# A 2048-cube matmul with layer norm: the first four row tiles cut one quarter to three quarters along k, and the row means of B written one tile earlier

## The chip, the cores and the metric

The kernel runs on one core of a Trainium2 chip. The metric is device time in microseconds (us) for one execution of the whole program. The engines named below: PE multiplies matrices, DVE (VectorE) and ACT (ScalarE) work elementwise, POOL (GpSimd) here mostly issues DMAs, SP (SyncE) only issues DMAs. PE writes into PSUM, which has eight banks of 128 x 512 f32; DVE and ACT move results out of it.

## The reference

```python
x = np.matmul(a, b)                     # a, b: 2048 x 2048 f32
mean = np.mean(x, axis=-1, keepdims=True)
var = np.var(x, axis=-1, keepdims=True)
normalized = (x - mean) / np.sqrt(var + eps)
return (gamma * normalized + beta).astype(np.float32)
```

## The kernel before

A is cut into 16 row tiles of 128 rows (i or g), k into 16 blocks of 128 (kt or t), the columns of B into four groups of 512 (q; q 0 and 1 are the left half, 2 and 3 the right). One product of PE (`mm`, L136 to L140) multiplies one k block of one row tile, transposed, with 512 columns of B into one PSUM bank. There are 15 x 4 x 16 = 960 of them; the last row tile is done apart with other widths (`products_last`, L219).

All data come as f32 and are cast to f16. B comes in half rows: `load_b(kt, h)` (L74) loads 128 x 1024 f32 (512 KB) of k block kt, left (h 0) or right (h 1), into one of eight slots (`bigp`), named w{kt}_{h}. `cast_left` and `cast_right` (L79, L84) cast 512 columns each on DVE and ACT into the resident `b16`, which frees the slot.

The first four row tiles (G = 4) are handled apart, since PE could otherwise do little until all of B is there. Their A comes in 16 pieces n of 128 rows x 512 of k (256 KB), four row tiles for each quarter c of k: `load_first(n)` (L91) loads it into a slot of `firstp` (four slots, each as large as half a row tile), `cast_first` (L97) casts it on DVE, `turn_first` (L102) transposes it on PE into a PSUM bank (four small matmuls), `keep_first` (L107) copies it from there on DVE into `at[g]`. The later row tiles come as two halves of eight DMAs of 64 KB (`load_tile`, L111), are cast on ACT (`cast_tile`, L119) and transposed on DVE (`transpose_part`, L127).

Four row tiles times two column groups fill the eight banks, and one bank is needed for the pieces being transposed. So the start goes in four stages: left columns over k blocks 0 to 7, right columns over 0 to 7, left columns over 8 to 15, right columns over 8 to 15. In the first two, seven banks (`early`) are filled while the pieces are transposed through the eighth; then the eighth (`late`) is filled too. `put_by` (L147) copies a bank's half sum to SBUF on ACT (f32, 16 copies in all), which frees the bank for the next stage; `add_up` (L151) in the last two stages adds the second part to it on DVE; `stats` (L142) then takes the statistics.

After that each row tile goes through all of k for four banks in turn (L442 to L460), DVE takes statistics, centres and scales (`normalise`, L184), SP stores. The results of the first four tiles are normalised beside the products of tiles 4 to 11.

The last tile needs its row mean early. For that the row means of B are appended to b16 as two more columns: `sum_b` (L206) sums the rows of b16 on ACT during tiles 6 to 13, `mean_b` (L211) makes of it, with four small DVE instructions and 16 small ACT copies (L217), the columns N and N+1 of b16, which the first products of the last tile read.

The order on every engine is the order of the program text (a schedule written out by hand). Each engine works in order, so an instruction that waits holds back all behind it on its engine. A DMA on a queue waits for the slot it fills and for the DMA eight before it in the program. At the very start PE does products on zeros (`warm_up`, L297) as fillers.

Of the kernel before, what the change touches and what calls it, by code (L numbers as in the profile page):

```python
# [15 lines left out]
def kernel(  # L16
# [57 lines left out]
    def load_b(kt, h, queue=None):  # L74
        w = bigp.tile([P, NH], FP32, tag="big", name=f"w{kt}_{h}")
        (queue or nc.sync).dma_start(w, b_rows[kt // 4, kt % 4][:, ds(h * NH, NH)])
        b_in[kt, h] = w
# [12 lines left out]

    def load_first(n):  # L91
        g, c = pieces[n]
        f = firstp.tile([P, 4 * P], FP32, tag="first", name=f"f{g}_{c}")
        nc.sync.dma_start(f, a[ts(g, P), ts(c, 4 * P)])  # L94
        a_in[n] = f

    def cast_first(n):  # L97
        h = first16.tile([P, P, 4], FP16, tag="h", name=f"h{n}")
        nc.vector.tensor_copy(h.rearrange("m p t -> m (p t)"), a_in[n])  # L99
        a_in[n] = h  # L100

    def turn_first(n):  # L102
        t_of[n] = psum.tile([P, 4, P], FP16, tag="c_ps", bufs=8, name=f"t_ps{n}")
        for t in range(4):
            nc.tensor.transpose(t_of[n][:, t, :], a_in[n][:, :, t], ident)  # L105
# [5 lines left out]
    def load_tile(i, h, queue):  # L111
        f = firstp.tile([P, 2, 4, P], FP32, tag="first", name=f"p{i}_{h}")
        for c in (0, 1):
            for q in range(4):
                queue.dma_start(  # L115
                    f[ds(32 * q, 32), c], a_pieces[q, 2 * h + c][:, ds(4 * i, 4)])
        tile_in[i, h] = f
# [6 lines left out]
    def new_at(i):  # L124
        at[i] = atp.tile([P, n_kt, P], FP16, tag="at", name=f"at{i}")
# [7 lines left out]
    def bank(i, q):  # L133
        x_of[i, q] = psum.tile([P, NB], FP32, tag="c_ps", bufs=8, name=f"ps_{i}_{q}")
# [11 lines left out]

    def put_by(i, q):  # L147
        part[i, q] = xpool.tile([P, NB], FP32, tag="x_sb", name=f"x_{i}_{q}")
        nc.scalar.copy(part[i, q], x_of[i, q])  # L149

    def add_up(i, q):  # L151
        x = part[i, q]
# [138 lines left out]
    with tc.manual_schedule(engines=order):  # L291
        nc.vector.memset(warm, 0.0)
        nc.vector.memset(ident, 0.0)
        nc.vector.memset(eps_t, float(eps))
        w_ps = psum.tile([P, NB], FP32, tag="c_ps", bufs=8, name="w_ps")

        def warm_up(n):  # L297
            for _ in range(n):
                nc.tensor.matmul(w_ps, warm[:, 0:P], warm, start=True, stop=True)

        nc.gpsimd.affine_select(
            out=ident, in_=ident, compare_op=AluOp.not_equal, fill=1.0,
            base=0, pattern=[[-1, P]], channel_multiplier=1,
        )
        KH = n_kt // 2
        load_first(0)
        load_b(0, 0, nc.scalar)
        load_first(1)
        for n in range(1, KH):
            load_first(n + 1)  # L310
            load_b(n, 0)
        for t in range(KH):
            load_b(t, 1)
            if KH + t + 1 < n_kt:
                load_first(KH + t + 1)
        for t in range(KH, n_kt):
            load_b(t, 0)
        for t in range(KH, n_kt):
            load_b(t, 1)
        for i in (4, 5):  # L320
            for h in (0, 1):
                load_tile(i, h, nc.sync)
        nc.sync.dma_start(gamma_b, gamma.unsqueeze(0).to_broadcast([P, N]))
        nc.sync.dma_start(beta_b, beta.unsqueeze(0).to_broadcast([P, N]))
        for i in range(6, n_mt):
            for h in (0, 1):
                load_tile(i, h, nc.gpsimd)

        left = [(g, q) for g in range(G) for q in (0, 1)]
        right = [(g, q) for g in range(G) for q in (2, 3)]  # L330
        early, late = left[:-1], left[-1]
        for g in range(G):
            new_at(g)


        warm_up(10)
        cast_first(0)
        turn_first(0)
        cast_first(1)
        warm_up(2)  # L340
        for n in range(KH):
            g, c = pieces[n]
            keep_first(n)
            cast_left(n)
            cast_first(n + 2)
            if n + 1 < KH:
                turn_first(n + 1)
            if n in (0, 1, 2):
                warm_up((3, 3, 2)[n])
            if c == 0:  # L350
                for x in early:
                    if x[0] == g:
                        bank(*x)
            if n == KH - 1:
                break
            for t in range(g + 1):
                for gg, q in early:
                    if gg <= g and (gg == g or t == g):
                        mm(gg, q, 4 * c + t, 0, KH)
        bank(*late)  # L360
        cast_right(0)
        for g, q in early:
            for t in range(4 if g == 3 else KH - 1, KH):
                mm(g, q, t, 0, KH)
            put_by(g, q)
            if (g, q) == (1, 1):
                cast_right(1)
        for t in range(KH):
            mm(*late, t, 0, KH)
        cast_right(2)  # L370
        put_by(*late)


        early, late = right[:-1], right[-1]
        for g, q in early:
            bank(g, q)
        for t in range(KH):
            n = KH + t
            turn_first(n)
            if t > 2:  # L380
                cast_right(t)
            keep_first(n)
            if n + 2 < n_kt:
                cast_first(n + 2)
            if t < KH - 2:
                for g, q in early:
                    mm(g, q, t, 0, KH)
        bank(*late)
        for t in range(KH, KH + 2):
            cast_left(t)  # L390
        for g, q in early:
            for t in (KH - 2, KH - 1):
                mm(g, q, t, 0, KH)
            put_by(g, q)
        for t in range(KH):
            mm(*late, t, 0, KH)
        put_by(*late)
        for t in range(KH + 2, n_kt):
            cast_left(t)


        for g, q in left:
            bank(g, q)
        for t in range(KH, KH + 3):
            for g, q in left:
                mm(g, q, t, KH)
        for j, (g, q) in enumerate(left):
            for t in range(KH + 3, n_kt):
                mm(g, q, t, KH)
            add_up(g, q)  # L410
            if j % 2 and j < 6:
                cast_right(KH + j // 2)


        for g, q in right:
            bank(g, q)
        for t in range(KH + 3, n_kt):
            cast_right(t)
            stats(*left[t - KH - 3])
        for g, q in left[5:]:  # L420
            stats(g, q)
        for t in range(KH, n_kt - 2):
            for g, q in right:
                mm(g, q, t, KH)
        new_at(4)
        for h in (0, 1):
            cast_tile(4, h)
            transpose_part(4, 2 * h)
            transpose_part(4, 2 * h + 1)
        for g, q in right:  # L430
            for t in (n_kt - 2, n_kt - 1):
                mm(g, q, t, KH)
            add_up(g, q)
        for g, q in right:
            stats(g, q)
        new_at(5)
        for c in range(4):
            if c % 2 == 0:
                cast_tile(5, c // 2)
            transpose_part(5, c)  # L440

        for i in range(G, last):  # L442
            if i == 6:
                junk = xpool.tile([P, 2 * NB], FP16, tag="x_sb", name="junk")
            if i > G:
                normalise(i - 1)
            if i + 2 < n_mt:
                new_at(i + 2)
            for q in range(n_nb):
                bank(i, q)  # L450
                for t in range(n_kt):
                    mm(i, q, t)
                stats(i, q)
                if i + 2 < n_mt:
                    if q % 2 == 0:
                        cast_tile(i + 2, q // 2)
                    transpose_part(i + 2, q)
                if 6 <= i < 14:
                    sum_b(4 * (i - 6) + q, junk)
                if q == 3 and i < 3 * G:  # L460
                    normalise((i - G) // 2, (i - G) % 2)
        mean_b()
        normalise(last - 1)
        for j in range(len(spans)):
            products_last(j)
            if j == 0:
                mean_last()
            stats_last(j)
            if j < len(spans) - 2:
                centre_last(j)  # L470
        finish_last()
# [31 lines left out]
```

## Time and profile before

| | us |
|---|---|
| median of 17 runs | 249.21 |
| lowest, highest | 248.43, 250.97 |
| the profiled execution | 248.33 |
| its span in the profile | 246.4 |
| PE busy (of the span) | 232.6 (94%) |
| DVE busy | 194.3 (79%) |
| ACT busy | 96.0 (39%) |

The span runs from the first to the last instruction of the profiled execution. "Busy" of PE counts fillers and the waits inside a run of pipelined products, so it isn't PE at its peak: a product shows as 379 ns each, and yet they follow each other faster. In the lists a group's line (L137) is that of the helper that issued it, `out<-in` are the program's tile names, "x960" is a count, and "idle before" is what its engine waited just ahead of it and for whom. The chain of work is followed back from the last instruction: at each step to what released it.

### The profile page before, as it was taken

The page shows a single profiled execution, that of the slowest core. Times are in us where ns is not written, and L with a number is a line of the kernel's source. Part 1 is how long each engine was busy: PE and PEld are TensorE (multiplying, and loading weights), DVE is VectorE, ACT ScalarE, POOL GpSimd, SP SyncE. Part 2 cuts the span into 40 slices and gives each one's busy share as a digit, 9 for nine tenths or more (in the row PEclk, how much of TensorE's full clock was granted, in tenths as well). Part 3 has the DMA queues.
Part 4 walks back from the last instruction along what each step waited for, and adds up shares of the span by engine and source line. Part 5 has one row for each costly group of instructions (what it writes and reads, how often), then busy time and mean ns, then how long its engine had stood idle before and what let it go on. Part 6 is the DMA issues. An engine that isn't in the chain of part 4 may idle for free.

```text
span 246.4 us, 3406 instructions
## 1 busy us (share of the span) xinstructions
PE 232.6 (94%) x1140; PEld 108.8 (44%) x1140; DVE 194.3 (79%) x365; ACT 96.0 (39%) x173; POOL 89.0 (36%) x168
## 2 busy tenths in 40 slices
PE   6899999999999999999999999999999999997960
PEld 2444454444444444444444444444444444445440
DVE  1664464379799799998999899998999894927962
ACT  2235637643216130461909264461909290002020
POOL 0000000000885498788956708692850000000011
PEclk9999999999999999999999999999999999999995
DMA  6999999995799758584865526472664230220404
GB/s 185 398 399 401 402 405 410 407 394 126 195 216 297 182 169 276 180 259 132 261 199 216 210 113 237 162 282 79 228 186 170 85 138 35 85 85 0 173 0 170
DMA packets 22129, 52.66 MB, mean 214 GB/s; under 512 B 4448, under 2 KB 9056, under 8 KB 21856
## 3 DMA queue, kind: packets, MB, share of 16 engines
q1 hardware_dynamic: 16560, 41.21, 46.1%
q0 software_dynamic: 5120, 10.50, 16.1%
q10 hardware_dynamic: 432, 0.74, 0.9%
q8 instruction: 9, 0.15, 0.3%
q14 instruction: 8, 0.07, 0.1%
HBM read 35.65 MB, written 16.78 MB: 213 GB/s over the span
## 4 chain that ended last, share of the span: by engine, by line
PE 84%; DMA 8%; ACT 2%; DVE 2%; DVEq 0%; issue 0%; SPq 0%
PE ps L137 78%; PE ps_last L223 6%; DMA f<-in_a_dram 5%; DMA w<-in_b_dram 3%; ACT x L149 2%; PE t_ps L105 1%; ACT b L87 1%; DVE c L280 1%; DVE bnst L145 0%; DVEq L498 0%; DVE at L109 0%; DVE h L99 0%; DVE ps_last L252 0%; SPq L94 0%; DVE mv_last L265 0%
## 5 line engine op out<-in xcount | busy, mean ns | idle before, releaser
L137 PE MATMUL ps<-b,at 128*128 128x512 f16 x960 | 209.9, 379 | 0.2
L137 PEld LDWEIGHTS <-at 128*128 128x128 f16 x960 | 93.5, 98 | 111.2 <-issue 0.7
L115 POOL DMA_DIRECT2D p<-in_a_dram x160 | 86.9, 550 | 94.4 <-DMA p<-in_a_dram 72.9
L176 DVE SCALAR_TENSOR_TENSOR c<-u,rs,beta_b 128x512 f32<-128x512 f32 x60 | 42.2, 743 | 0.0
L145 DVE BATCH_NORM_STATS2 bnst<-ps 128x6 f32<-128x512 f32 x44 | 29.7, 678 | 13.1 <-PE ps L137 13.1
L208 ACT ACTIVATE junk<-b 128x1024 f16<-128x1024 f16 x32 | 33.7, 1054 | 0.5
L128 DVE STREAM_TRANSPOSE at<-a 128x512 f16<-128x512 f16 x48 | 32.6, 686 | 1.3 <-ACT a L121 1.3
L160 ACT ACTIVATE sq<-mv,eps_t 128x1 f32<-128x1 f32 x15 | 4.4, 294 | 72.0 <-DVE mv L158 72.0
L170 DVE SCALAR_TENSOR_TENSOR u<-ps,mv,gamma_b 128x512 f32<-128x512 f32 x44 | 31.6, 742 | 0.4
L121 ACT CAST a<-p 128x1024 f16<-128x1024 f32 x24 | 24.7, 1039 | 13.7 <-DMA p<-in_a_dram 13.7
L262 POOL TENSOR_TENSOR u_last_n<-u_last_n,gamma_b 128x128 f32<-128x128 f32 x1 | 0.5, 453 | 56.0 <-ACT u_last_n L261 56.0
L82 ACT CAST b<-w 128x512 f16<-128x512 f32 x16 | 9.7, 633 | 16.8 <-DMA w<-in_b_dram 16.8
L223 PE MATMUL ps_last<-b,at 128*128 128x512 f16 (+4 forms) x96 | 14.1, 308 | 1.7 <-ACT b L217 1.7
L87 ACT CAST b<-w 128x512 f16<-128x512 f32 x16 | 10.0, 624 | 13.3 <-DMA w<-in_b_dram 13.3
L99 DVE CAST h<-f 128x512 f16<-128x512 f32 x16 | 6.8, 423 | 9.1 <-DMA f<-in_a_dram 9.1
L81 DVE CAST b<-w 128x512 f16<-128x512 f32 x16 | 6.8, 425 | 8.2 <-DMA w<-in_b_dram 8.1
L153 DVE TENSOR_TENSOR x<-ps,x 128x512 f32<-128x512 f32 x16 | 10.4, 681 | 3.1 <-PE ps L137 2.9
L223 PEld LDWEIGHTS <-at 128*128 128x128 f16 x96 | 8.8, 98 | 7.3 <-issue 2.0
L170 DVE SCALAR_TENSOR_TENSOR u<-x,mv,gamma_b 128x512 f32<-128x512 f32 x16 | 11.4, 735 | 0.1
L109 DVE COPY at<-t_ps 128x512 f16<-128x512 f16 x16 | 6.7, 421 | 5.2 <-PE t_ps L105 5.0
L145 DVE BATCH_NORM_STATS2 bnst<-x 128x6 f32<-128x512 f32 x16 | 10.0, 676 | 0.0
L105 PE MATMUL t_ps<-ident,h 128*128 128x128 f16 x64 | 6.2, 220 | 2.4 <-DVE h L99 1.5
(38 smaller groups left out, 59.4 us busy)
## 6 DMA issues: line engine op xcount, KB each, us to landing
w<-in_b_dram SPq DMA_DIRECT2D x31, 512.0 KB, 8.5
out_dram<-c SPq DMA_DIRECT2D x30, 512.0 KB, 3.1
p<-in_a_dram POOLq DMA_DIRECT2D x160, 64.0 KB, 3.8
f<-in_a_dram SPq DMA_DIRECT2D x16, 256.0 KB, 7.2
p<-in_a_dram SPq DMA_DIRECT2D x32, 64.0 KB, 3.9
gamma_b<-in_gamma_dram SPq DMA_DIRECT2D x1, 1024.0 KB, 9.3
beta_b<-in_beta_dram SPq DMA_DIRECT2D x1, 1024.0 KB, 12.9
w<-in_b_dram ACTq DMA_DIRECT2D x1, 512.0 KB, 5.1
```

The costliest lines, as they stand in the source:

```text
L82: nc.scalar.copy(b16[:, kt, NB:NH], w[:, NB:NH])
L87: nc.scalar.copy(b16[:, kt, NH + NB:N], w[:, NB:NH])
L115: queue.dma_start(f[ds(32 * q, 32), c], a_pieces[q, 2 * h + c][:, ds(4 * i, 4)])
L121: nc.scalar.copy(a16, tile_in.pop((i, h)))
L128: nc.vector.transpose(at[i][:, ds(4 * c, 4), :].rearrange("p t (j r) -> p j t r", r=32), tile_in[i, c // 2][:, c % 2].rearrange("p j (k t) ...
L137: nc.tensor.matmul(x_of[i, q], at[i][:, kt, :], b16[:, kt, ds(q * NB, NB)], start=(kt == lo), stop=(kt == hi - 1),)
L145: nc.vector.bn_stats(bnst[i][:, q, :], x_of[i, q])
L153: nc.vector.tensor_tensor(x, x_of[i, q], x, AluOp.add)
L170: nc.vector.scalar_tensor_tensor(u, x_of[i, q], mv_of[i][:, 0:1], gamma_b[:, ds(q * NB, NB)], AluOp.subtract, AluOp.mult,)
L176: nc.vector.scalar_tensor_tensor(c[:, ds(q % 2 * NB, NB)], u, rs_of[i], beta_b[:, ds(q * NB, NB)], AluOp.mult, AluOp.add,)
L208: nc.scalar.activation(junk, b16[:, kt, ds(h * NH, NH)], ActFn.Copy, accum_out=b_sum[:, h, kt:kt + 1])
L223: nc.tensor.matmul(x[:, 0:w], at[last][:, t, :], b16[:, t, ds(lo, w)], start=(t == 0), stop=(t == n_kt - 1))
```

## The change

Three things are changed.

1. The cut of the first four row tiles along k is at block 4 (K1), not at block 8 (KH). The four stages are now: left over 0 to 3, right over 0 to 3, left over 4 to 15, right over 4 to 15. The loads, casts, transposes and products of these stages are put in a new order to match, the first half row of B (w0_0) is asked for by SP and no longer by ACT, and the first half of tile 4 is asked for ahead of the last two right half rows. The left columns over 4 to 15 now carry the transposes of pieces 8 to 15.
2. Of the 16 copies of `put_by`, those of odd column groups go to DVE, the others stay on ACT. Two pieces of A share one slot of `firstp`, so that eight are in flight.
3. `mean_b` stands after `normalise(13)` at the head of tile 14, not after tile 14.

The diff, cut to its core:

```diff
     def load_first(n):
         g, c = pieces[n]
-        f = firstp.tile([P, 4 * P], FP32, tag="first", name=f"f{g}_{c}")
-        nc.sync.dma_start(f, a[ts(g, P), ts(c, 4 * P)])
-        a_in[n] = f
+        if n % 2 == 0:
+            a_in[n + 1] = firstp.tile([P, 2, 4 * P], FP32, tag="first", name=f"f{g}_{c}")
+            a_in[n] = a_in[n + 1][:, 0]
+        else:
+            a_in[n] = a_in[n][:, 1]
+        nc.sync.dma_start(a_in[n], a[ts(g, P), ts(c, 4 * P)])
...
     def put_by(i, q):
         part[i, q] = xpool.tile([P, NB], FP32, tag="x_sb", name=f"x_{i}_{q}")
-        nc.scalar.copy(part[i, q], x_of[i, q])
+        if q % 2:
+            nc.vector.tensor_copy(part[i, q], x_of[i, q])
+        else:
+            nc.scalar.copy(part[i, q], x_of[i, q])
...
-        KH = n_kt // 2
-        load_first(0)
-        load_b(0, 0, nc.scalar)
-        load_first(1)
-        for n in range(1, KH):
-            load_first(n + 1)
-            load_b(n, 0)
-        for t in range(KH):
+        K1 = 4
+        for t in range(K1):
+            load_first(t)
+            load_b(t, 0)
+        for t in range(K1):
             load_b(t, 1)
-            if KH + t + 1 < n_kt:
-                load_first(KH + t + 1)
-        for t in range(KH, n_kt):
+            if t:
+                load_first(K1 + t - 1)
+        load_first(2 * K1 - 1)
+        for t in range(K1, n_kt):
             load_b(t, 0)
-        for t in range(KH, n_kt):
+            if K1 + t < n_kt:
+                load_first(K1 + t)
+        for t in range(K1, n_kt - 2):
             load_b(t, 1)
-        for i in (4, 5):
-            for h in (0, 1):
-                load_tile(i, h, nc.sync)
+        load_tile(4, 0, nc.sync)
+        for t in range(n_kt - 2, n_kt):
+            load_b(t, 1)
+        load_tile(4, 1, nc.sync)
+        for h in (0, 1):
+            load_tile(5, h, nc.sync)
...
         warm_up(10)
         cast_first(0)
         turn_first(0)
-        cast_first(1)
-        warm_up(2)
-        for n in range(KH):
...
+        warm_up(3)
+        for n in range(K1):
             keep_first(n)
             cast_left(n)
-            cast_first(n + 2)
...
+            if n < K1 - 1:
+                cast_first(n + 1)
+            for x in early:
+                if x[0] == n:
+                    bank(*x)
+            todo = [
+                (g, q, t) for t in range(n + 1) for g, q in early
+                if g <= n and (g == n or t == n)
+            ]
+            if n == K1 - 1:
+                break
+            ahead = (2, 4, 6)[n]
+            for x in todo[:ahead]:
+                mm(*x, 0, K1)
+            if n == 0:
+                warm_up(2)
+            turn_first(n + 1)
+            for x in todo[ahead:]:
+                mm(*x, 0, K1)
+            if n < 2:
+                warm_up(2)
         bank(*late)
-        cast_right(0)
-        for g, q in early:
-            for t in range(4 if g == 3 else KH - 1, KH):
-                mm(g, q, t, 0, KH)
+        for g, q, t in todo[:K1 - 1]:
+            mm(g, q, t, 0, K1)
+        waits = list(range(K1))
+        for j, (g, q) in enumerate(early):
+            mm(g, q, K1 - 1, 0, K1)
             put_by(g, q)
...
+            if j in (1, 3, 5):
+                mm(*late, waits.pop(0), 0, K1)
+            if j == 3:
+                cast_right(0)
+        for t in waits:
+            mm(*late, t, 0, K1)
         put_by(*late)
+        cast_right(1)
...
+        for t in range(K1 - 1):
+            if t:
+                keep_first(K1 + t - 1)
+                cast_right(t + 1)
+            cast_first(K1 + t)
+            for g, q in early:
+                mm(g, q, t, 0, K1)
+            if t < 2:
+                turn_first(K1 + t)
         bank(*late)
+        cast_first(2 * K1 - 1)
+        waits = list(range(K1))
+        for j, (g, q) in enumerate(early):
+            mm(g, q, K1 - 1, 0, K1)
+            put_by(g, q)
+            if j in (4, 6):
+                n = K1 + j // 2
+                turn_first(n)
+                keep_first(n)
+            if j in (1, 3, 5):
+                mm(*late, waits.pop(0), 0, K1)
+            if j == 2:
+                cast_left(K1)
+        for t in waits:
+            mm(*late, t, 0, K1)
+        put_by(*late)
...
+        for t in range(K1, n_kt - 3):
+            n = K1 + t
+            if t > K1:
+                keep_first(n - 1)
+            if n < n_kt:
+                cast_first(n)
+            cast_left(t + 1)
+            for g, q in early[:5]:
+                mm(g, q, t, K1)
+            if n < n_kt:
+                turn_first(n)
+            for g, q in early[5:]:
+                mm(g, q, t, K1)
+        bank(*late)
+        for t in range(n_kt - 2, n_kt):
             cast_left(t)
+        for t in range(K1, n_kt - 3):
+            mm(*late, t, K1)
         for j, (g, q) in enumerate(left):
-            for t in range(KH + 3, n_kt):
-                mm(g, q, t, KH)
+            for t in range(n_kt - 3, n_kt):
+                mm(g, q, t, K1)
             add_up(g, q)
             if j % 2 and j < 6:
-                cast_right(KH + j // 2)
+                cast_right(K1 + j // 2)
...
+        new_at(4)
+        for t in range(K1 + 3, n_kt):
+            if t == n_kt - 2:
+                cast_tile(4, 0)
+                transpose_part(4, 0)
+                transpose_part(4, 1)
             cast_right(t)
...
+        cast_tile(4, 1)
+        for j, (g, q) in enumerate(right):
             for t in (n_kt - 2, n_kt - 1):
-                mm(g, q, t, KH)
+                mm(g, q, t, K1)
             add_up(g, q)
+            if j in (1, 3):
+                transpose_part(4, 2 + j // 2)
...
             if i > G:
                 normalise(i - 1)
+            if i == last - 1:
+                mean_b()
...
-        mean_b()
         normalise(last - 1)
```

## The prediction

> **What bounds the kernel now.** I read the chain of work first. It is in order of time: start, length, what.
>
> ```profile
> 7.78 6.06 DMA f<-in_a_dram
> ...
> 13.91 8.47 DMA w<-in_b_dram
> ...
> 23.02 1.94 ACT x L149 x4
> 24.96 0.52 ACT b L87
> 25.48 1.46 ACT x L149 x3
> ...
> 37.96 184.34 PE ps L137 x854
> 222.29 0.02 issue
> 222.31 0.70 DVE bnst L145
> 223.01 0.08 DVE b_mean L212
> ...
> 223.76 0.20 ACT b L217
> 223.96 0.04 issue
> 224.00 14.08 PE ps_last L223 x96
> ```
>
> Loads set the pace up to 22.4 us, ACT's copies out of PSUM then hold PE a while, and from 37.96 to 222.29 PE does 854 products without a hole: 184.34 / 854 = 215.9 ns each. Then PE stands still until 224.00, for the row means of B. Next the stages (span of the stretch, PE busy, its weight loads, DVE, ACT, POOL, clock, DMA share, GB/s):
>
> ```profile
> 5.50:13.20 7.70, 6.23 (x40) 3.25 (x41) 4.56 (x12) 1.86 (x3) 0.00 (x0) 1.00 1.03 393
> ...
> 30.00:37.80 7.80, 7.28 (x52) 3.93 (x49) 5.08 (x14) 2.68 (x5) 0.00 (x0) 1.00 1.04 408
> ...
> 222.30:224.00 1.70, 0.00 (x0) 0.00 (x0) 1.55 (x7) 0.24 (x3) 0.00 (x0) 1.00 0.00 0
> ```
>
> The DMA engines are full (393 to 408 GB/s) while PE's "busy" hides fillers. Of the 960 products of L137, 854 lie after 37.96, so 106 lie before it, 106 x 0.2159 = 22.9 us; the 16 transposed pieces add 16 x 0.22 = 3.5. So 11.4 us before 37.8 are no useful PE work. Most of that is the wait for the first data; about 4 us are at stake, and 1.7 at 222.3. The groups give the prices (line, engine, tile, shape, count | busy, mean ns | idle before):
>
> ```profile
> L153 DVE TENSOR_TENSOR x<-ps,x 128x512 f32<-128x512 f32 x16 | 10.4, 681 | 3.1 <-PE ps L137 2.9
> L81 DVE CAST b<-w 128x512 f16<-128x512 f32 x16 | 6.8, 425 | 8.2 <-DMA w<-in_b_dram 8.1
> L109 DVE COPY at<-t_ps 128x512 f16<-128x512 f16 x16 | 6.7, 421 | 5.2 <-PE t_ps L105 5.0
> L149 ACT COPY x<-ps 128x512 f32<-128x512 f32 x16 | 8.3, 614 | 0.0
> ```
>
> Starts of neighbours in the timeline give the pitch in a row of such work: 0.34 us for the DVE casts, 0.605 for L153 (eight in 4.84), 0.50 for L149 (eight in 4.00).
>
> **When data land.** Casts released by DMA show w3_0 landed at 13.2 with 3.25 MB asked for up to it (f0 to f4, four half rows of B) and w7_0 at 21.1 with 6.25 MB: 2.63 us per MB. Total order by bytes is what counts, as the engines are full. In the changed order w0_0 ends 0.75 MB, w3_0 3.0 MB, w4_0 6.5 MB, w12_0 12.5 MB, w15_0 14 MB, so 6.6, 12.5, 21.7, 37.5 and 41.4 us. The trace passed 14 MB (w11_0) at 42.1, so the last may be 0.7 later. Here the skill has something to say: w0_0 moves from ACT's queue to SP's. In the trace it landed by 5.9, not 6.6. The Trainium skill, DMA: Bandwidth & Descriptors, section Queues, rings and completion order, has each DMA engine take turns between the queues with work, which is why a load alone on ACT's queue jumps the line. By the rule and the row w0_0 loses 0.7 us; by bytes, w3_0 loses nothing. I take 6.6.
>
> **Start, part by part.** After w0_0 and its cast (0.65) at 7.3, PE has ahead of the first product that needs w3_0: 2 + 6 + 10 + 3 = 21 products, three turns (turn_first 1 to 3) and 6 fillers (warm_up): 21 x 0.216 + 3 x 0.25 + 6 x 0.216 = 6.6, so 13.9. w3_0 is cast at 13.2, so PE, not the load, decides; the fillers cost 1.3 of it. From 13.9:
> - First stage's end: 11 products, 2.4, to 16.3. Behind it four evictions each on ACT and DVE and cast_right(0). What a DVE copy of f32 out of PSUM costs, no row shows. Nearest by name is L109 (421 ns, f16), nearest by data is L153 (681 ns, f32). The Trainium skill, VectorE: DVE Perf Modes, section Mode 2x_2P, says that a one-source f32 copy doubles its rate only between SBUF operands, PSUM having one read port. L81 (SBUF) and L153 (PSUM) fit that; by L109 eight copies would cost 8 x 0.34 = 2.7 of DVE, by the rule 8 x 0.605 = 4.8. I take 0.65 a copy; both ends stay for the range, 0.34 (L81's pitch) and 0.70 (two of L170, the dearest reader of PSUM, take 1.40). Below nothing it can't be: what ACT is spared, 8 x 0.50, is counted in the hand-overs already. DVE then ends its fourth copy 3.1 after the stage's decisive point, casts w1_1 (0.4), h4 (0.4): turn 4 is late by 0.35 behind seven products. Waiting behind these copies on DVE are cast_right, cast_first, keep_first; PE waits for those.
> - Second stage (right, k 0 to 3): 32 products, 6.9, 4 turns, 0.9, and that stall: 8.2 us, to 24.5. w3_1 lands at 19.1, in time. At its end four DVE copies, two casts and two keep_first stand before h8, turn 8 is late by 0.35 again.
> - Third (left, k 4 to 15): PE needs 7 x 0.216 + 0.22 = 1.73 us for each k block, the load of one half row and one piece 1.96. PE begins w4_0 at 24.5 (landed 21.7), so it has 2.1 us in hand after the cast and loses 0.23 a block: at w12_0, 8 blocks on with the 0.35 of turn 8, it wants the cast at 38.7, and has it at 38.2. Then that block, 1.5, 9 products of the late bank, 1.9, and two more: w15_0 is wanted at 42.5. It is cast by 42.1, or 42.8 by the trace's own 14 MB. Cost 0 to 0.3, 0.1 taken. With 24 products for the last three blocks the end is 47.4.
> - Fourth (right): eight add_up at 0.605 and three casts, 5.9 of DVE, against 24 products, 5.2. They release banks in the order PE takes them; PE's eighth product there needs the eighth at about the same moment. 0 to 0.3. 96 products, 20.7: tile 4 begins at 68.1.
>
> Before, tile 4 begins at 37.79 + 150 x 0.2159 = 70.2. Gain 2.1; with the small stalls at their ends 1.3, with none 2.9.
>
> Priced at nothing: pairs of pieces in one slot (eight in flight, not four; SP waited for slots before, but the DMA engines were full, so nothing is won, and f8 needs only f1's cast at 7.8). The first half of tile 4 is asked for before w14_1: eight small DMAs on SP, where each DMA waits for the one eight before it. In the trace 32 such took 22.5 us to issue, so eight delay w14_1 and w15_1 by up to 5.6, from some 55 to 60.6; PE wants w14_1 at 64.6. Its ACT cast (1.04) and two DVE transposes (1.29 as a pair) stand before cast_right(14); the same margin, 4 us less 2.3, covers them.
>
> **The row means.** mean_b (four DVE instructions, 16 on ACT) moves from after tile 14 to after tile 13 is normalised. The last b_sum is ready at about 203, the tile runs from 208.5 to 222.3, DVE is idle 2.1 us before the next statistics, ACT 13.5 (its row L217). 0.8 on DVE, 1.6 on ACT, hidden. PE's last product starts at 221.9, the next would start 0.216 later at 222.1, not at 224.0: 1.9 gained. What is late next? The last tile's own chain: DVE does statistics and normalise(14), about 0.6 + 5.6 (tile 13 shows 209.74 to 215.34), and begins mean_last some 6.4 after PE's start; before, it was 230.28 - 224.00 = 6.3, since sq waited 0.9 behind L217's copies. DVE idles 2.6 before the end, so the tail after the last product keeps its length.
>
> **Sum.** 2.1 + 1.9 = 4.0 against the profiled execution: 248.33 (span 246.4 and 1.9 around it) becomes 244.3. The median of 17 runs is 249.21, 0.9 above the profiled one; I carry that over: 245.2.
>
> **Rivals.**
> - *Hand-overs eat the start's gain.* DVE now carries copies that ACT had; if copies at their upper price with semaphore delays cost 1 us at each of two changes of bank set, or the loads arrive at the trace's later pace, the start gains 0.3 and only the means pay: 249.2 - 2.2 = 247.0. For it: turns and casts queue behind copies. Against: DVE is busy 4.6 of 7.7 us there. Chance 0.2.
> - *More than that.* DVE copies at 0.34 remove both 0.35 stalls, w0_0 lands at 5.9 and moves everything by 0.5: gain 5.2, 244.0. Against: PSUM f32 rows above. Chance 0.1.
> - *Slower: the clock falls in the first 14 us.* The trace's ten first fillers take 4.29 us, 0.43 each, later ones 0.216. The Trainium skill, TensorE: Matmul & The Clock Gate, Part 1, says that PE falls to half rate after an idle window of some 3.4 us and needs as much busy time to recover. The changed start has one filler less and other waits. Each lapse costs ten products x 0.216 = 2.2 us; from the second on the gain is gone, three give 249.2 - 4.0 + 6.6 = 251.8. Against: the longest gap worked out above is under 1 us, and the row 5.50:13.20 with gaps of 0.8 keeps 1.00. Chance 0.05, with 0.02 for w14_1 coming 4 us past PE's need.
> - *It does nothing,* because another wait (a bank held by tile 13) keeps PE after tile 14 and the start stalls too. Bank order gives the last tile those of tile 13, free at 215. Chance 0.03.
>
> **Numbers.** Forecast 0.6. A measurement here tells 0.2% (0.5 us) from no change. Faster 0.9, same 0.03, slower 0.07. The range takes in the forecast with its ends (1.3 to 2.9 at the start: 246.0 to 244.4) and both faster rivals: 243.9 to 247.2.
>
> **What would show it.** After: no PE idle between L137 and the last tile's products; mean_b's rows near 216; tile 4's first product near 68; DVE's PSUM copies at 600 to 680 ns; GB/s near 400 up to 50 us; PE clock 1.00. It is wrong if turn 4 or 8 waits over 0.5 us for DVE, if PE in the third stage waits for w, if w14_1 lands after 64, or if the first products take 0.43.

## The result and the profile after

The changed kernel takes 244.70 us (median of 8 runs, 244.6 to 244.87) where the kernel before takes 249.07 (47 runs, 248.14 to 250.97). The ratio is 0.9822, 95% interval 0.9805 to 0.9839: 4.0 to 4.9 us faster. The profiled execution took 244.6 us and its span is 242.8 (before 248.33 and 246.4). So the span is 3.6 shorter, and the median 4.4. Why the two differ is told below: the runs of the kernel before scatter over 2.8 us, those of the changed one over 0.3.

The chain of work of the changed kernel (start, length, what):

```profile
0.74 4.61 DMA f<-in_a_dram
5.38 0.44 DVE h L102
...
12.61 1.96 PE ps L140 x9
14.59 1.34 DVE x L153 x2
...
17.79 0.34 DVE h L102
18.18 0.42 PE t_ps L108 x4
...
25.20 0.60 DVE x L153
25.79 0.34 DVE h L102
26.18 0.41 PE t_ps L108 x4
...
38.74 181.89 PE ps L140 x842
220.63 13.92 PE ps_last L229 x96
```

Before, three links of 6.1 to 8.5 us of DMA led up to 22.4. Now one load, f0, stands at the head, and from 5.38 on the chain is PE with DVE in between. Twice DVE decides: at 14.59 to 18.18 and before 26.18 its copies out of PSUM (L153) stand ahead of a cast (h) that a transpose (t_ps, called turn 4 and turn 8 after its piece) waits for. From 38.74 on PE is the chain up to the end of the last tile's products (L229), which follow at once; before, they had to wait. PE's timeline gives the starts of these, before and after:

```profile
224.00 14.07 PE L223 MATMUL ps_last<-b,at 128*128 128x290 f16 x96 [1.73 <-ACT b L217]
220.46 14.07 PE L229 MATMUL ps_last<-b,at 128*128 128x290 f16 x96
```

The stages, for the same two stretches as before (length, PE busy, its weight loads, DVE, ACT, POOL, clock, DMA share, GB/s):

```profile
5.50:13.20 7.70, 7.05 (x43) 3.42 (x44) 4.41 (x12) 2.47 (x4) 0.00 (x0) 1.00 1.04 412
30.00:37.80 7.80, 7.80 (x51) 4.09 (x49) 5.41 (x14) 2.48 (x4) 0.00 (x0) 1.00 1.03 403
```

PE is busy all through 30.00 to 37.80 (7.28 of 7.80 us before), with the DMA engines as full as before. The clock is 1.00 in both stretches.

The groups that copy half sums out of PSUM (line, engine, tile, shape, count | busy, mean ns | idle before):

```profile
L153 DVE COPY x<-ps 128x512 f32<-128x512 f32 x8 | 5.4, 684 | 1.7 <-PE ps L140 1.7
L155 ACT COPY x<-ps 128x512 f32<-128x512 f32 x8 | 4.5, 587 | 3.9 <-PE ps L140 3.7
```

A DVE copy of f32 from PSUM takes 684 ns, as the row of the addition (681) had it and not as that of the f16 copy (421). The addition has two sources, so its row alone couldn't tell what a copy with one costs; this row does. And the timeline of ACT, whose casts start when the data land (idle before and for whom, in brackets):

```profile
38.48 0.62 ACT L82 CAST b<-w 128x512 f16<-128x512 f32 x1 [1.31 <-DMA w<-in_b_dram]
...
60.25 0.62 ACT L87 CAST b<-w 128x512 f16<-128x512 f32 x1 [0.90 <-DMA w<-in_b_dram]
...
214.53 1.59 ACT L223 COPY b<-b_hilo 128x2 f16<-128x2 f16 x16 [5.89 <-DVE b_hilo L221]
```

w12_0 landed at 38.48, w14_1 at 60.25, and the row means are written at 214.53 to 216.1, 4.5 us ahead of their use.

### The profile page after: what moved, and what is told of

Read it like the earlier page. It is cut to its first block, busy times and chain, and to the rows that moved or that the text cites. A ratio compares the mean times of both kernels' runs of the same rounds, so it can differ in the third digit from the quotient of the medians.

```text
span 242.8 us, 3393 instructions
## 1 busy us (share of the span) xinstructions
PE 231.6 (95%) x1139; PEld 108.2 (45%) x1139; DVE 198.2 (82%) x373; ACT 92.8 (38%) x165; POOL 89.2 (37%) x168
## 4 chain that ended last, share of the span: by engine, by line
PE 91%; DVE 5%; DMA 2%; issue 0%; DVEq 0%
PE ps L140 83%; PE ps_last L229 6%; DVE x L153 2%; DMA f<-in_a_dram 2%; PE t_ps L108 2%; DVE c L286 1%; DVE at L112 1%; DVE h L102 0%; PE w_ps L305 0%; DVE b L81 0%; DVE b L86 0%; DVEq L536 0%; DVE ps_last L258 0%; DVE mv_last L271 0%; DVE bnst_last L248 0%
## 5 line engine op out<-in xcount | busy, mean ns | idle before, releaser
L229 PE MATMUL ps_last<-b,at 128*128 128x512 f16 (+4 forms) x96 | 14.1, 308 | 0.0
L87 ACT CAST b<-w 128x512 f16<-128x512 f32 x16 | 9.8, 621 | 10.3 <-DMA w<-in_b_dram 10.3
L112 DVE COPY at<-t_ps 128x512 f16<-128x512 f16 x16 | 6.8, 422 | 6.8 <-PE t_ps L108 6.7
L229 PEld LDWEIGHTS <-at 128*128 128x128 f16 x96 | 8.8, 98 | 5.4
L108 PEld LDWEIGHTS <-h 128*128 128x128 f16 x64 | 5.1, 114 | 5.9 <-DVE h L102 3.5
```

The source lines that it names most:

```text
L229: nc.tensor.matmul(x[:, 0:w], at[last][:, t, :], b16[:, t, ds(lo, w)], start=(t == 0), stop=(t == n_kt - 1))
```

## The experiments

My theory ahead of them: the row means pay 1.9 and the start some 2, and these add; the start also takes away the kernel's scatter, since PE no longer follows each load; in the third stage loads and PE are now level. Rivals: one of the two parts does most of it; the scatter belongs to two queues at the start; the gain comes from where the copies run.

The runs were made in three groups of four, in the order below. Each ratio is to the kernel before, run in the same group (medians 249.67, 249.21 and 249.47). The changed kernel was not run again in them; three versions in which nothing was gained or lost came out at 244.62 to 244.76, so its 244.70 can be compared to about 0.1.

**The row means alone**, all else as before:

```diff
             if i > G:
                 normalise(i - 1)
+            if i == last - 1:
+                mean_b()
...
-        mean_b()
         normalise(last - 1)
```

> The kernel before, with mean_b moved to the head of tile 14 and nothing else. Theory (two gains that add, and a start set by PE instead of by loads also ends the scatter from run to run): 1.8 us below the kernel before, median 247.3, and its runs scatter over 2 us as those of the kernel before do (248.1 to 251.0). Rival (the scatter belongs to the wait at the end, on ACT and DVE): runs within 0.5 us of each other, median nearer 246.5. Rival (one gain hides in the other): under 1 us gained.

Measured: 247.34 us (9 runs, 246.47 to 248.41), ratio 0.9921, interval 0.9894 to 0.9949. The hole is gone, and the runs scatter as before. The end of its chain:

```profile
31.07 9.58 DMA w<-in_b_dram
...
40.67 0.62 ACT b L82
41.29 3.91 ACT x L149 x8
...
45.25 178.22 PE ps L137 x825
223.47 13.92 PE ps_last L223 x96
```

The span of this execution is 245.7, only 0.7 under that of before, although the hole (1.7) is missing. The lines show why: here w9_0 landed at 40.67 (38.87 in the profiled execution of before), its cast on ACT stands ahead of the eight evictions (the copies of `put_by`), and PE has its last 825 products from 45.25; before it was at the same product at 37.96 + 29 x 0.216 = 44.22. So 1.0 us of a late landing reached the end in this execution.

**The start alone**, with the row means where they were:

```diff
-            if i == last - 1:
-                mean_b()
...
+        mean_b()
         normalise(last - 1)
```

> The changed kernel with mean_b back after tile 14. Theory: the start alone gives 1.8 us in the profiled span (span near 244.6) and a narrow scatter, within 0.5 us, so the median gains 2.6, to 246.5. Rival (scatter belongs to the end): the runs scatter over 2 us, median 247.3. The hole before the last tile's products is again 1.7 us.

Measured: 246.61 us (6 runs, 246.28 to 246.81), ratio 0.9892, interval 0.9863 to 0.9922. The hole is back, 1.68 us from the end of the products (220.82) to the last tile's first:

```profile
220.82 0.70 DVE bnst L148
...
222.50 14.08 PE ps_last L229 x96
```

The two ratios multiply to 0.9814, inside the interval of the whole change (0.9805 to 0.9839): within the noise the parts add. The narrow scatter (0.5 us) comes with the new start and not with the row means.

**w0_0 on ACT's queue in the changed kernel**, since before it landed by 5.9 there:

```diff
         for t in range(K1):
             load_first(t)
-            load_b(t, 0)
+            load_b(t, 0, nc.sync if t else nc.scalar)
```

> The changed kernel with the first half row of B asked for on ACT's queue again. By the trace of the kernel before it lands near 5.9 and not at 6.6. Theory (PE sets the start from there on): the first product comes 0.5 to 0.7 earlier and 0.3 to 0.5 of it are kept, median 244.3, unless w3_0 (cast at 13.1) becomes the limit. Rival (the scatter of the kernel before comes from two queues sharing the DMA engines at the start): its runs scatter over 2 us.

Measured: 244.98 us (6 runs, 244.93 to 245.17), ratio 0.9828, interval 0.9799 to 0.9857. The expected gain did not come. The head of its chain:

```profile
0.74 5.20 DMA f<-in_a_dram
5.97 0.44 DVE h L102
```

w0_0 landed at 6.30 instead of 6.64, but the two loads now share the DMA engines, and f0 came at 5.97 instead of 5.38. The first product needs f0's cast, transpose and copy too, and went from 7.13 to 7.71. The scatter stays small: two queues at the start don't make it.

**The reverse in the kernel before**, w0_0 on SP's queue:

```diff
-        load_b(0, 0, nc.scalar)
+        load_b(0, 0)
```

> The kernel before with the first half row of B on SP's queue behind the first piece of A. Theory (loads pace its start by total bytes): within 0.3 us of the kernel before, median 249.1, with the same scatter over 2 us. Rival (two queues at the start make the scatter): runs within 0.5 us, median near 248.4.

Measured: 249.66 us (12 runs, 248.25 to 250.65), ratio 1.0, interval 0.9973 to 1.0027, with the scatter of before. The queue of w0_0 is no part of the gain that can be told.

**Evictions first in the kernel before**: the casts of w8_0 and w9_0 are put behind the seven evictions on ACT, so that a late w9_0 no longer holds them up (the place that the row-means run pointed to):

```diff
-        for t in range(KH, KH + 2):
-            cast_left(t)
         for g, q in early:
             for t in (KH - 2, KH - 1):
                 mm(g, q, t, 0, KH)
             put_by(g, q)
+        for t in range(KH, KH + 2):
+            cast_left(t)
```

> The kernel before with the casts of w8_0 and w9_0 put behind the seven evictions of the right columns on ACT and DVE, and not ahead of them. Theory (the kernel before scatters because ACT's eight evictions stand behind the cast of w9_0, which landed at 38.9 in its own profile, but at 40.7 and 41.0 in those of the two variants with its start): median 248.3, which is the level of its best executions, and a scatter below 1 us. Rival (the scatter comes from the loads of the first 25 us): unchanged, median 249.5 and 2 us of scatter.

Measured: 249.15 us (12 runs, 248.44 to 249.99), ratio 0.9994, interval 0.9971 to 1.0017. My theory of one cause for the scatter fell: the median stayed, and the range, 2.5 us for the kernel before beside it, is still 1.55. Its chain has another load in it:

```profile
29.88 6.99 DMA f<-in_a_dram
...
38.62 184.34 PE ps L137 x854
```

PE's 854 products begin 0.66 later than in the profile of before, this time because of a piece of A. So more than one place of this start passes a late landing on.

The four profiles with the old start (the kernel before, this run and the two variants above) show where loads come late. Counted from w7_0, bytes (2.75 MB at 2.63 us each) give w3_1 7.2 us later; it landed 7.4 later in the kernel before and here, 8.0 in the row-means run and 8.6 in the run with w0_0 on SP. The stretch from 33 to 37 us differs too, here the kernel before and then the run with w0_0 on SP (columns as above, GB/s at the end):

```profile
33.00:37.00 4.00, 4.00 (x28) 2.23 (x27) 2.18 (x6) 1.27 (x3) 0.00 (x0) 1.00 1.03 408
33.00:37.00 4.00, 4.00 (x26) 2.10 (x25) 1.99 (x6) 1.24 (x2) 0.00 (x0) 1.00 1.01 340
```

The other two have 358 and 338 GB/s there. In all four SP waits up to 2.4 us for the cast of a piece whose slot it needs, and in the three it goes on to the next half rows 0.5 to 0.7 us later than in the kernel before (30.1 to 30.3 for 29.63). So the full DMA engines belong to that profiled execution, which was a lucky one. That the loads' landing makes the scatter is read off four executions; no run isolates it.

**No fillers after the first ten** in the changed kernel, for the rival of the clock and for the time of these nine (9 x 0.216 = 1.9 us):

```diff
-        warm_up(3)
...
-            if n == 0:
-                warm_up(2)
...
-            if n < 2:
-                warm_up(2)
```

> The changed kernel without the nine fillers after the first ten. Theory A (PE sets the pace from 7 to 68 us): 0.7 us less, since then w3_0's cast at 13.1 sets the start of the rest in place of 13.9: median 244.0. Theory B (the loads are level with PE at w12_0, cast at 39.1 where PE wants it at 39.0): within 0.2 us of the changed kernel, 244.6, and the first products come earlier in the profile all the same. Rival (clock): PE falls to half rate before 14 us, products at 0.43, 246 or more.

Measured: 244.65 us (median of 6 runs), ratio 0.9848, interval 0.9802 to 0.9894. Four runs lie at 244.33 to 244.78, two at 246.86 and 247.39. The profiled execution is the last of these. Its stages (columns as above; the clock is the third from the right):

```profile
4.60:8.00 3.40, 1.59 (x9) 0.54 (x7) 1.19 (x3) 0.62 (x1) 0.00 (x0) 1.00 0.99 378
8.00:10.00 2.00, 0.95 (x5) 0.48 (x6) 1.18 (x3) 0.62 (x1) 0.00 (x0) 0.50 1.02 401
...
14.00:16.00 2.00, 2.00 (x12) 0.95 (x11) 0.56 (x2) 0.00 (x0) 0.00 (x0) 0.79 1.04 405
```

and the gaps around the fall, from PE's timeline:

```profile
5.82 0.41 PE L108 MATMUL t_ps<-ident,h 128*128 128x128 f16 x4 [0.64 <-DVE h L102]
7.09 0.59 PE L140 MATMUL ps<-b,at 128*128 128x512 f16 x2 [0.85 <-DVE b L81]
8.53 0.62 PE L108 MATMUL t_ps<-ident,h 128*128 128x128 f16 x4 [0.85 <-DVE h L102]
```

PE's clock was halved from 8.0 to about 14.8 us (0.79 is the mean over 14 to 16), after gaps of 0.64 and 0.85 and while a third of 0.85 ran. The changed kernel, with its fillers, has PE busy for 2.38 of the same 3.40 us and keeps the clock:

```profile
4.60:8.00 3.40, 2.38 (x15) 0.96 (x13) 1.61 (x4) 0.62 (x1) 0.00 (x0) 1.00 1.03 407
```

So the rival of the clock is real without fillers, and none of the changed kernel's 8 runs shows such a loss. The run of 246.86 has no profile, and its mean clock of 0.988 is that of undisturbed runs (the profiled one has 0.975), so its cause is not shown. In the four other runs (median 244.50) nine fillers less gained some 0.2, and not the 0.7 of theory A; that PE then meets the loads fits the runs further below.

**All half-sum copies on ACT** in the changed kernel:

```diff
-        if q % 2:
-            nc.vector.tensor_copy(part[i, q], x_of[i, q])
-        else:
-            nc.scalar.copy(part[i, q], x_of[i, q])
+        nc.scalar.copy(part[i, q], x_of[i, q])
```

> The changed kernel with all 16 evictions on ACT. Theory (the split over DVE carries the shorter stages): each of the two hand-overs is longer by 0.8 to 1 us, the loads hide none of it, median 246.3. Theory B (loads level with PE at w12_0): the first 0.1 us is free, the rest is paid as well. Rival (DVE was the late engine in the hand-overs, turn 4 and turn 8 waited for it): without its copies these turns are in time and the median is 244.7 or below.

Measured: 245.65 us (6 runs, 245.53 to 246.32), ratio 0.9863, interval 0.9834 to 0.9892. About 1.0 slower than the changed kernel, and than the run below, made beside it (244.62). Its chain shows ACT at both changes of bank set:

```profile
14.54 2.05 ACT x L152 x4
...
17.10 1.97 ACT x L152 x4
...
25.14 2.45 ACT x L152 x5
```

So the share of DVE is worth 1.0 of the start's gain. What is left belongs to the new cut, the orders that go with it and the slots in pairs; the cut and the orders were not run apart.

**Casts of pieces 4 and 8 earlier** in the changed kernel, ahead of the DVE copies that make turns 4 and 8 late:

```diff
         for t in waits:
             mm(*late, t, 0, K1)
+        cast_first(K1)
         put_by(*late)
         cast_right(1)
...
-            cast_first(K1 + t)
+            if t:
+                cast_first(K1 + t)
...
                 turn_first(n)
                 keep_first(n)
+                if j == 4:
+                    cast_first(2 * K1)
...
-            if n < n_kt:
+            if K1 < t and n < n_kt:
                 cast_first(n)
```

> The changed kernel with the casts of pieces 4 and 8 ahead of the last evictions on DVE, so that turn 4 and turn 8 don't wait for them (0.33 and 0.58 us in the profile). Theory A (PE sets the pace): median 243.8. Theory B (loads level with PE at w12_0): PE arrives earlier and waits for w12_0, 244.5 to 244.7.

Measured: 244.62 us (6 runs, 243.88 to 244.8), ratio 0.9813, interval 0.978 to 0.9845: no gain that can be told. Turn 8 came 0.84 earlier (25.34 for 26.18). PE's timeline in the third stage shows where it went, by the starts of the last turns:

```profile
34.30 0.39 PE L108 MATMUL t_ps<-ident,h 128*128 128x128 f16 x4
...
36.27 0.39 PE L108 MATMUL t_ps<-ident,h 128*128 128x128 f16 x4
...
38.20 0.39 PE L108 MATMUL t_ps<-ident,h 128*128 128x128 f16 x4
```

They stand 1.97 and 1.93 us apart, the pace of the loads (1.96 for a half row and a piece), not PE's own 1.73. The chain says it too; up to the last products it now consists of loads:

```profile
30.85 7.73 DMA w<-in_b_dram
...
38.60 0.44 DVE b L81
...
39.08 181.62 PE ps L140 x840
```

The changed kernel has 840 products left at 39.17 (38.74 and two products), so 0.1 of the lead is kept.

**The same two kernels with lighter loads**: pieces 8 to 15 of A are not loaded (pieces 6 and 7 are used again), which takes 2 MB out of the third stage and leaves all instructions of PE, DVE and ACT. These two kernels leave out that part of A.

```diff
         g, c = pieces[n]
+        if n >= 8:
+            a_in[n] = a_in["kept"][:, n % 2]
+            return
         if n % 2 == 0:
             a_in[n + 1] = firstp.tile([P, 2, 4 * P], FP32, tag="first", name=f"f{g}_{c}")
+            if n == 6:
+                a_in["kept"] = a_in[7]
             a_in[n] = a_in[n + 1][:, 0]
```

The changed kernel with it:

> The changed kernel, but the pieces of A from number 8 on (k from 1024, first four row tiles) are not loaded; the two pieces 6 and 7 are cast and transposed in their place, so 2 MB of loads fall out of the third stage and all instructions of PE, DVE and ACT stay. Left out: that part of A. My theory: in the third stage loads and PE's own work are level, PE losing only about 0.15 us to the casts of w12_0 to w15_0 and 0.6 to turn 8, which is DVE's. So 244.5 us (244.3 to 244.7), the products without a hole from about 38.4. Rival, loads set the pace of the third stage alone (each block 1.96 us of loads against 1.73 of PE): then their lightening gives some 1 us, 243.6.

Measured: 244.76 us (5 runs, 244.38 to 244.87), ratio 0.9806, interval 0.9777 to 0.9835. No gain: loads alone do not hold the changed kernel back. From the first product to the point at which 842 products are left it takes 31.52 us (7.40 to 38.92), the changed kernel 31.61 (7.13 to 38.74).

The version with the earlier casts:

> The same lightening (pieces 8 to 15 of A not loaded, that part of A left out), on the version that casts pieces 4 and 8 earlier. With full loads that version had PE 0.85 us earlier in the third stage and lost all of it to late landings. My theory (loads and PE level, each covering the other's gain): now the 0.85 is kept, 243.8 us (243.6 to 244.1), the products without a hole from about 37.7 instead of 38.4. Rival, the early casts gain nothing for a reason of DVE or PE itself: 244.5 as without them.

Measured: 244.19 us (5 runs, 243.89 to 244.39), ratio 0.9785, interval 0.9756 to 0.9814. Now the earlier casts are worth 0.57 us against the line above, measured side by side. PE's timeline, the same three turns:

```profile
34.22 0.39 PE L113 MATMUL t_ps<-ident,h 128*128 128x128 f16 x4
...
35.95 0.39 PE L113 MATMUL t_ps<-ident,h 128*128 128x128 f16 x4
...
37.69 0.39 PE L113 MATMUL t_ps<-ident,h 128*128 128x128 f16 x4
```

They stand 1.73 and 1.74 apart. I had expected 243.8; the 0.85 was the lead of turn 8, while the products behind it lead by 0.61 (31.00 us from the first product to the same point, 7.08 to 38.08, against 31.61). Of these 0.61, full loads leave 0.1, and light ones all. Lightening alone gains nothing, earlier casts alone gain nothing, both together gain 0.6: loads and PE are level in the third stage.

**One piece of A to a slot**, four in flight instead of eight:

```diff
-        if n % 2 == 0:
-            a_in[n + 1] = firstp.tile([P, 2, 4 * P], FP32, tag="first", name=f"f{g}_{c}")
-            a_in[n] = a_in[n + 1][:, 0]
-        else:
-            a_in[n] = a_in[n][:, 1]
+        a_in[n] = firstp.tile([P, 4 * P], FP32, tag="first", name=f"f{g}_{c}")
```

> The changed kernel with one piece of A to a slot, so four in flight and not eight. The prediction priced this part at nothing, since the DMA engines are full: 244.7 us within 0.2. Rival: SP waits for a slot until an early piece is cast, the loads queued behind it on SP come later, and as the third stage has no slack on its loads, up to 1 us is lost: 245.5.

Measured: 245.1 us (6 runs, 244.78 to 245.98), ratio 0.9825, interval 0.9793 to 0.9856. 0.4 slower than the run below, made beside it, but not in every run: three lie at 244.78 to 244.84, as the changed kernel, and three at 245.36 to 245.98. The profiled execution (245.62) is one of the latter. The waits of SP's queue (waited for: us in total, times, longest) hold two that the changed kernel hasn't got or has at 0.3:

```profile
SPq L94 <- DVE b L81: 5.1, 4, 2.2
SPq L94 <- DVE h L98: 4.3, 3, 2.4
```

and its stages move less in the third stage, where the changed kernel moves 401 and 404 GB/s:

```profile
24.50:31.00 6.50, 6.06 (x38) 2.99 (x36) 5.05 (x14) 2.51 (x5) 0.00 (x0) 1.00 1.01 378
31.00:38.50 7.50, 7.18 (x46) 3.69 (x44) 4.40 (x12) 2.17 (x4) 0.00 (x0) 1.00 1.02 376
```

SP stands at a load of A until a slot's earlier piece is cast (L98), and half rows of B are queued behind it. PE then waits for casts of w in the third stage (0.32 and 0.18 us). Some 25 GB/s less over these 14 us are 0.9 us of loads, and this execution's span (243.8) is 1.0 longer.

**Row tile 4 asked for last**, as before:

```diff
-        load_tile(4, 0, nc.sync)
         for t in range(n_kt - 2, n_kt):
             load_b(t, 1)
+        load_tile(4, 0, nc.sync)
```

> The changed kernel with the first half of row tile 4 asked for after the last right half row, as in the kernel before. The prediction priced the place at nothing: w14_1 then lands some 3 us earlier than 60.25 and the half tile after 61; its cast on ACT stands ahead of the cast of w14_1, needed at 64.9, and is done by 63. 244.7 us within 0.2. Rival: the half tile comes after 63, cast_right(14) and with it the fourth stage's end wait: 245.5 or more.

Measured: 244.69 us (5 runs, 244.66 to 244.94), ratio 0.9809, interval 0.9781 to 0.9837: the same. ACT's timeline:

```profile
60.80 1.04 ACT L124 CAST a<-p 128x1024 f16<-128x1024 f32 x1 [4.95 <-DMA p<-in_a_dram]
61.75 1.13 ACT L87 CAST b<-w 128x512 f16<-128x512 f32 x2
```

The half tile comes at 60.80 instead of 58.31, its cast and those of w14_1 and w15_1 (L87) are done by 62.9, and PE wants them at 64.9.

## Why the prediction held, and which terms were off

*Mechanism.* The row means' hole and the start's lost PE time were named as the two gains, and they are: each part alone gains its share, and within the noise they add. One of the prediction's own signs of being wrong did appear, since turn 8 waited 0.6 us for DVE where it had set the bound at 0.5. That cost some 0.25 us and did not undo the mechanism; none of the other signs appeared.

*First products.* First product at 7.13 (7.3 in the prediction), w0_0 at 6.64 (6.6), w3_0 at 12.49 (12.5), the first product that needs it at 13.96 (13.9). Summing bytes over full DMA engines worked up to here, and so did the choice of 6.6 for w0_0.

*DVE's copies.* 684 ns each and 0.60 to 0.66 from one to the next, 0.65 taken. Turn 4 was late by 0.33 (0.35). The third stage begins at 24.5 as said, but turn 8 was late by 0.6, not 0.35: the prediction named the two copies of transposed pieces (L112, 0.33 and 0.41 us in the chain) that stand ahead of its cast in addition, and yet took turn 4's number.

*Third stage.* PE's period of 1.73 is right. The landing times were mis-sized: w12_0 landed at 38.48, not at 37.5, and w6_0 already at 26.76 where bytes give 25.7; w3_1 was in time (19.00 for 19.1). So 1 us was lost between 19 and 27, though the engines moved 400 GB/s. It cost nothing here, since turn 8's lateness had used up the same time: w12_0's halves are cast by 38.91 (DVE) and 39.10 (ACT), the products that want them start at 39.01 and 39.22, and PE's timeline has no gap from there into the fourth stage. The 0.1 taken for w12_0 to w15_0 was not needed. The light-load run of the changed kernel agrees.

*Fourth stage.* Its eighth product starts at 49.31, 0.37 after the one ahead and not 0.216, just when DVE has done the last of the eight additions (two from 47.98, to 49.26). The prediction had named this wait at 0 to 0.3 and left it out of the sum; it is 0.16.

*Tile 4* begins at 68.5 (704 products ahead of 220.46) and not at 68.1: the start gains 1.7 there, not 2.1.

*Priced at nothing.* For the order of tile 4's first half that was right (244.69 with it put back; w14_1 at 60.25 was within the margin to 64.9). For the pairs of pieces it was wrong by 0.4 in the median, 0.1 to 1.3 from run to run: the full DMA engines of one execution were taken as proof that more pieces in flight win nothing. With one piece to a slot, a slot comes free later than the next load is due, and SP stops with B queued behind it.

*Row means.* Written at 214.53 to 216.1 ("near 216"), no hole. The last tile starts 3.54 earlier (220.46 for 224.00); the products ahead of it end 1.66 earlier (220.63 for 222.29), so 1.9 is this part's own (1.9 in the prediction). The last tile's own chain took 6.58 us to mean_last (6.4), and PE's end to the end of the span stayed 8.3: nothing new became late.

*The sum.* 1.7 and 1.9 make the span's 3.6, where 4.0 was said; turn 8 (0.25 more than taken) and the fourth stage's wait (0.16) are the missing 0.4. The other way lay the step "I carry that over": the median of before stood 0.9 above its profiled execution because that execution was one of its luckiest, and I added the 0.9 to a kernel which has no such scatter (its median is 0.1 above its profiled one). So 0.4 of gain too much and 0.8 of offset too much made 245.2 of what was measured as 244.7. The two errors partly cancel, and that the forecast came within 0.5 us is to that extent luck.

*Rivals.* Hand-overs that eat the gain: DVE's share of the copies is what keeps them small (1.0 worse without). Half clock: not here, but seen in a run without fillers. The lower copy price and w0_0 at 5.9: neither; w0_0 on ACT's queue costs 0.3.

What stays open is the 1 us of the loads between 19 and 27 (last section), which no run isolates, and what the cut at block 4 is worth without the new orders.

## What to carry to other kernels

Before a profiled execution's distance to the median is carried over to a changed kernel, ask what makes the scatter and whether the change takes it away; then the median gains more than the profiled span. Here the old start, whose chain runs through several loads, scattered by 1.6 to 2.8 us, and the new one, a chain of PE and DVE, by 0.2 to 0.5. Loads in the chain are not enough, though: the run with earlier casts has them up to 38.6, and five of its six runs lie within 0.2. Where two limits are level (here the loads, which start early and take 1.96 us a block, and PE, which starts later and takes 1.73), easing either alone shows nothing, and only both together show what each is worth. Full DMA engines in one profiled execution do not make buffers in flight worthless: the price of fewer has to be worked out for the new order of issue, with what is queued behind the load that waits.

## What the hardware showed that was not expected

- Half clock without a long gap. In the run without fillers the granted clock fell to 0.50 at 8.0 us and stayed there until 14.8. Ahead of the fall stand gaps of 0.64 and 0.85 us, and a third had begun; PE was busy for 1.59 of the 3.40 us up to it. The Trainium skill, TensorE: Matmul & The Clock Gate, Part 1, speaks of an idle window of about 3.4 us, and the prediction read that as "no single gap that long". The rows decide: several short gaps in a stretch of that length, under half busy, were enough in this execution. How busy PE has to be was not measured; 2.38 of 3.40 kept the clock.
- Loads that land 1 us late at full GB/s. In the changed kernel's DMA view of the stretch from 23 to 24 us there is one packet that is none of the kernel's data (queue and kind: packets, MB, share of 16 engines):

```profile
q8 instruction: 1, 0.02, 6.9%
```

  6.9% of 16 engines over 1 us is 1.1 us of one engine. If a half row is spread over all engines, it is complete only when that one has caught up, which would fit the loss of 1 us between 19 and 27. The GB/s rows fit a delay of that kind and not a lower rate: by them (an estimate) the engines had moved 0.45 MB more than the loads up to w3_1 when that landed, and 0.9 MB more than those up to w6_0 when that did, so later loads had gone ahead of w6_0's last bytes. But the packet alone doesn't explain it. The kernel before has the same one from 22 to 23, and in its profile w3_1 landed at 28.49, within 0.2 us of what bytes give from w7_0; in the run with w0_0 on SP, with a packet of 6.4% at 21 to 22, 1.3 us were lost. The Trainium skill, Runtime: NRT & Kernel Launch, Instruction fetch mechanics, has sequencers fetch blocks of instructions over DMA queues of their own and calls the cost mostly hidden; no run here shows what such a packet costs, and the cause stays open.
- Two queues share the engines in the first microseconds: w0_0 on ACT's queue came 0.34 us earlier and f0 on SP's 0.59 later.
